# Attention's low parts stored apart and added later by DMA; the last bias of the fourth token block added in PSUM

## The chip, the core and the metric

The kernel runs on one core of a Trainium2 chip. Its engines are TensorE (PE, matmuls; PEld is its weight load), VectorE (DVE), ScalarE (ACT), GpSimd (POOL) and SyncE (SP, which only issues DMAs here). Each engine works through its own instructions in program order, and semaphores hold it where it needs what another has made. POOL issues DMAs as well, in line with its own arithmetic. Matmul results go to PSUM; everything else lies in SBUF, which DMAs fill from device memory.

The metric is the time of one execution on the device, in microseconds (us). Lower is better.

## The reference

One decoder layer in fp32, 512 tokens of width 2048, 16 query heads of 64 on 4 key heads, window 128:

```python
h = rms_norm(x, norm_gain[i])
z = h @ w_in[i]
q, k, v, g_attn, c_b, c_c, c_h, g_conv = jnp.split(z, SPLITS, axis=-1)
...
y_attn = sliding_window_attention(q, k, v, attn_sinks[i]) * jax.nn.silu(g_attn)
y_conv = c_b * short_conv(c_c * c_h, conv_w[i]) * jax.nn.silu(g_conv)
mix = jnp.concatenate([y_attn, y_conv], axis=-1)
x = x + mix @ w_out[i]
gate = jax.nn.sigmoid(rms_norm(x, ple_gate_norm_gain[i]) @ w_ple_gate[i] + b_ple_gate[i])
e = rms_norm(p[i] @ w_ple_proj[i], ple_norm_gain[i])
x = x + gate * e
```

Two places matter here: the sum of probabilities times values inside the attention, and the last line with the gate's bias `b_ple_gate`.

## The kernel before

**Precision.** Every fp32 operand is split into a high half, rounded to fp32r, and a low half, the rest. A product is three fp32r matmuls: high by high, low by high, high by low. `halves` makes a split: a cast on ACT (L199) and a subtraction on DVE (L200). The weight blocks so split are called wh and wl.

**Weight groups.** Most of the matrix work runs as nine groups g = 0 to 8 of `PER` = 28 steps, each step twelve 128x512 matmuls at L241: g 0 to 4 make the parts of the input projection (2 and 3 for the convolution, 4 for the attention's gate), 5 and 6 the output projection, 7 and 8 the gate of the per-layer embedding. A group computes a 2x2 product of blocks with seven products in place of eight, so weight blocks are first added to one another, on DVE (L189, L191) or by accumulating DMAs of POOL (L169). `run_step` does a step: the actions put in the table `before` for that step, the sums and splits of weight blocks ahead (`prepare(s + 2)`: two steps ahead, three pairs of buffers), the matmuls, the actions in the table `after`. `soon(table, s, fn, ...)` enters an action. That order of the code is the order of the engines.

**Attention.** It runs between 127 and 280 us, mixed with the matmuls of the remaining projections. `gemm_tile` (L712) calls `tick()` after every six of its matmuls, and `at(when, fn)` says at which tick a piece of the attention is issued. There are sixteen units, key head j by token block n. A unit's pieces are `scores` at its tick (matmuls L814 and L815, maxima and small 128x4 arithmetic on DVE, exponentials on ACT at L833), `turn` four ticks later (PE transposes the probabilities at L842, `halves` makes pth and ptl, and two POOL selects at L849 make the masked copies pph and ppl), `values` seven ticks later (four matmuls L859 onto pso, with pth, ptl, pph, ppl in that order), and one more twelve ticks later. In `values` ACT copies pso to `up`. Its upper 64 rows hold the product with the values' high halves and its lower 64 rows that with the low halves. POOL stores the upper rows to `attn_dram` (tiles a, L863); at tick 12 of the unit POOL issues a store of the lower rows that accumulates on the same place (L864). Five ticks ahead of every second unit `turn_q` turns the queries: PE transposes, `halves` makes `st` and `low`, and three POOL DMAs (L795 to L797) copy 64-row halves across partitions.

The result in `attn_dram` is first read in group 4, from step 18, by the loads of raw (563.8 to 587.7 us).

**The last two groups.** `token_scale`, in group 7 after its step 3, makes `r_2`, the reciprocal rms of each token: a sum and a scale on DVE (L309, L310), a power on POOL (L303). `gate_group` takes results out of PSUM (`take` L1294 on ACT, `join` L1302 on DVE), adds the bias, takes the sigmoid, multiplies by e (`times_e`, L1320), adds x2 and stores. In group 8 the block (t, n) = (1, 0), 128-token halves b = 0 and 1, comes last. Its products lie in two PSUM banks called pst. Its bias is added by `whole` (L1305): bank times r_2 plus gb, on DVE, in one 128x512 for b = 0 and two 128x256 for b = 1 (`tail`). Then come the sigmoid (L1382), `times_e`, the addition of x2 (L1375) and the store (L1376). The last two steps run all products of the first token half ahead of those of the second, with `first_block` (b = 0) between. `eps_tok` is a 128x4 tile that the attention stage uses and nothing reads later.

Where the program is written out, the scheduler keeps each engine's order in the weight groups as the tables give it. In the attention stage PE's order is by hand, and the other engines' order follows from what is ready.

Of the kernel before, what the change touches and what calls it, by code (L numbers as in the profile page):

```python
# [9 lines left out]
F32 = mybir.dt.float32  # L10
F32R = mybir.dt.float32r
AF = mybir.ActivationFunctionType
ALU = mybir.AluOpType
# [22 lines left out]
def hymba_layer(ctx: ExitStack, tc: tile.TileContext, io):  # L36
# [300 lines left out]
        soon(before, s0 + 21, lambda: join(qs[1, 1], g, "a", ALU.subtract))  # L337
        soon(after, s0 + 26, lambda: join(qs[0, 0], g, "c", ALU.add))

    attn_dram = [dram.tile([2 * P, T], F32, name=f"a{j}") for j in range(NKV)]  # L340
    conv_dram = [dram.tile([P, T], F32, name=f"c{i}") for i in range(4)]
    mix_dram = [dram.tile([P, T], F32, name=f"m{i}") for i in range(8)]
    tap_dram = [dram.tile([T, T], F32, name=f"t{i}") for i in range(3)]
# [439 lines left out]
    def turn_q(j, t):  # L783


        pt = ps_m.tile([P, T], F32, name="psm")
        for b in range(2):
            for f in range(2):
                s = j % 2 * 2 * P + f * P
                i = 2 * b + f  # L790
                nc.tensor.transpose(pt[:, i * P : (i + 1) * P], qs[t, j // 2][:, b, s : s + P], ident)
        st, st2 = (rowp.tile([P, T], F32R, tag="rows", name="st") for _ in range(2))
        low = misc.tile([P, T], F32R, tag="m", name="low")
        halves(st, low, pt)
        nc.gpsimd.dma_start(st2[:HD], st[HD:])  # L795
        nc.gpsimd.dma_start(st2[HD:], low[HD:])
        nc.gpsimd.dma_start(st[HD:], low[:HD])  # L797
        turned[j, t, 0], turned[j, t, 1] = st, st2

    turned = {}  # L800

    def attention(j, n, when):
# [52 lines left out]
        def values():  # L855
            po = ps_o.tile([P, 4, P], F32, name="pso")
            for i, (w, x) in enumerate(cell["pt"]):
                w = w.rearrange("p s d -> p (s d)")
                nc.tensor.matmul(po, w, x, start=i == 0, stop=i == len(cell["pt"]) - 1)  # L859
            up = mtile("up").rearrange("p (r t) -> p r t", t=P)  # L860
            nc.scalar.copy(up, po)
            rows = attn_dram[j].rearrange("(r d) (n t) -> d r n t", d=HD, n=NB)[:, :, n]
            nc.gpsimd.dma_start(rows, up[:HD])  # L863
            cell["add"] = lambda: nc.gpsimd.dma_start(rows, up[HD:], accum_op=ALU.add)  # L864

        if n % 2 == 0:
            at(when - 5, lambda: turn_q(j, n // 2))
        at(when, scores)
        at(when + 4, turn)
        at(when + 7, values)  # L870
        at(when + 12, lambda: cell["add"]())


    pgs = []
# [254 lines left out]
    def load_raw(j, src):  # L1129
        new_pair(mixf, j, move=j == 4)  # L1130
        for i in range(2):
            nc.sync.dma_start(pairs[id(mixf), j][0][i], src[(2 * j + i) % 8])

    attn_tiles = [attn_dram[i // 2][i % 2 * P : (i % 2 + 1) * P] for i in range(8)]

    def attn_group(g):
# [130 lines left out]
    for t in range(2):  # L1267
        soon(after, s1 + 5 + t, reload, t, 1)

    r_2, n_2 = [], []  # L1270

    def token_scale():
        r_2.append(inv_rms(x2sq, "x2"))
        n_2.append(const.tile([P, NB], F32, name="nr_x2"))
        nc.gpsimd.tensor_scalar(n_2[0], r_2[0], -1.0, None, op0=ALU.mult)

    soon(after, s2 + 3, token_scale)


    out = io["out"].rearrange("b p n -> p b n")  # L1280

    def gate_group(g):
        s0 = g * PER
        q, ext = {}, {}

        def load_b():
            ext["b"] = itile("gb")
            nc.sync.dma_start(ext["b"], io["b_ple_gate"][2 * (g - 7)][:, 0])

        def take(t, n, acc, r):  # L1290
# [10 lines left out]
            for b in range(2):  # L1301
                stt(z[:, b], psum[g, acc][b], column(r[0], t, b), z[:, b], op0=ALU.mult, op1=ALU.add)  # L1302

        def whole(t, n, b, cols=slice(0, T)):
            stt(  # L1305
                q[t, n][:, b, cols], psum[g, "a"][b][:, cols], column(r_2[0], t, b), ext["b"][:, cols],
                op0=ALU.mult, op1=ALU.add,
            )

        def load_e(t, n, tile=itile):  # L1310
            ext[t, n] = [tile("e") for _ in range(2)]
# [34 lines left out]
        soon(before, s0 + 21, join, 1, 1, "a", n_2)  # L1346
        finish(1, 1, s0 + 21)
        finish(0, 1, s0 + 20)
        soon(after, s0 + 22, load_b)
        soon(after, s0 + 22, load_e, 0, 0, itile if g == 7 else spare)  # L1350

        def new_z():
            q[1, 0] = qtile("z")

        if g == 7:
            soon(after, s0 + 26, join, 0, 0, "c", r_2)
            soon(after, s0 + 28, new_z)
            for b in range(2):
                soon(after, s0 + 28, whole, 1, 0, b)
            finish(0, 0, s0 + 28)  # L1360
            soon(after, s0 + 29, load_e, 1, 0)
            finish(1, 0, s0 + 31)
            return
# [3 lines left out]
            for b in range(2):  # L1367
                nc.sync.dma_start(ext["x2", t, n][b], x2_dram[t][2 + n][:, b])

        def piece(t, n, b, cols=slice(0, T), begun=False):  # L1370
            z = q[t, n][:, b, cols]
            if not begun:
                nc.scalar.activation(z, z, AF.Sigmoid)
            times_e(t, n, b, cols)
            tt(z, z, ext["x2", t, n][b][:, cols], op=ALU.add)  # L1375
            nc.sync.dma_start(part(out, t, 2 + n)[:, b, cols], z)  # L1376

        def tail(b, parts):
            cols = [slice(h * T // parts, (h + 1) * T // parts) for h in range(parts)]
            for c in cols:  # L1380
                whole(1, 0, b, c)
                nc.scalar.activation(q[1, 0][:, b, c], q[1, 0][:, b, c], AF.Sigmoid)  # L1382
            for c in cols:
                piece(1, 0, b, c, True)

        def first_block():
            new_z()
            tail(0, 1)

        soon(after, s0 + 21, load_x2, 0, 0)  # L1390
        soon(after, s0 + 22, load_x2, 1, 0)
        soon(after, s0 + 24, load_e, 1, 0, spare)
        soon(after, s0 + 24, join, 0, 0, "c", r_2)
        for b in range(2):
            soon(after, s0 + 25, piece, 0, 0, b)
        tail_work.append(first_block)
        soon(after, s0 + 27, tail, 1, 2)

    for g in T3_BY_DMA:
        for i, c in enumerate(chunks[g]):  # L1400
# [145 lines left out]
```

## Time and profile before

| | us |
|---|---|
| median of 3 runs | 914.39 (913.33 to 915.92) |
| profiled execution, device time | 912.85 |
| its span, first to last instruction | 911.1 |
| mean granted clock of PE | 0.998 |
| attention stage | 127 to 280 |
| last matmul starts | 904.51 |

Times below are counted from the start of the span. A page row of the engines gives busy time, its share and the number of instructions. A row of the timeline gives start, duration, engine, line, operation, output and inputs, and in brackets how long the engine had been idle before it and who released it. A row of waits gives the waiting instruction, who released it, and the sum in us, the number and the longest of such waits. "DMA x<-y" as a releaser is the landing of that transfer. Matmuls are pipelined: their recorded durations overlap, and their spacing is what one costs.

### The profile page before, as it was taken

To read this page: it belongs to the slowest core of one execution; us is meant where nothing else is said; L and a number is where in the kernel's file an instruction comes from. 1 tells how busy PE (TensorE), PEld (TensorE's weight loads), DVE (VectorE), ACT (ScalarE), POOL (GpSimd) and SP (SyncE) were. 2 spreads that over 40 slices of the span, in tenths; PEclk is the share of its full clock that TensorE was granted. 3 is DMA by queue.
4 is the path that set the end of the run, shared out by engine and by line. 5 is a ranking of instruction groups with operands and counts; after the bars stand their busy time and mean duration, and the time that the engine had idled before them with its cause. 6 is when DMAs were issued, how large, how long until landed. Compare 5 with 4: busy or idle time off the path is not lost.

```text
span 911.1 us, 11967 instructions
## 1 busy us (share of the span) xinstructions
PE 900.5 (99%) x4130; PEld 746.3 (82%) x4130; DVE 714.1 (78%) x967; ACT 527.7 (58%) x849; POOL 193.0 (21%) x264
## 2 busy tenths in 40 slices
PE   9999999999999999999999999999999999999997
PEld 7888888887878888888888888888888888888885
DVE  6878889887757687877768678997858887799678
ACT  6766848676653443454344457766556666665453
POOL 4232143376640001100130110012120112111100
PEclk9999999999999999999999999999999999999999
DMA  8999558756668858648478897858996995898647
GB/s 312 360 292 308 212 61 274 246 112 133 151 130 310 288 173 237 179 147 257 126 201 247 222 237 257 234 127 230 341 293 198 212 293 142 234 306 256 185 139 219
DMA packets 74445, 202.34 MB, mean 222 GB/s; under 512 B 8867, under 2 KB 15331, under 8 KB 74384
## 3 DMA queue, kind: packets, MB, share of 16 engines
q1 hardware_dynamic: 48672, 134.24, 43.1%
q0 software_dynamic: 25568, 67.33, 33.0%
q8 instruction: 32, 0.52, 0.2%
q14 instruction: 29, 0.24, 0.1%
q10 hardware_dynamic: 144, 0.01, 0.0%
HBM read 166.94 MB, written 31.46 MB: 218 GB/s over the span
## 4 chain that ended last, share of the span: by engine, by line
PE 86%; DVE 5%; issue 2%; ACT 2%; DMA 2%; POOL 2%; SPq 0%; DVEq 0%; POOLq 0%; ACTq 0%
PE psp L241 68%; PE psg L712 4%; PE pst L241 4%; PE psp L520 3%; PE pst L1024 2%; PE pss L900 1%; PE pst L1422 1%; PE pst L900 1%; DMA raw<-in_w_kv 1%; DVE wl L200 1%; DVE z L1320 1%; PE pso L859 1%; DMA st<-st 1%; DVE ptl L200 0%; DMA a<-up 0%
## 5 line engine op out<-in xcount | busy, mean ns | idle before, releaser
L241 PE MATMUL psp<-wh,form 128*128 128x512 f32 x1280 | 395.3, 390 | 0.0
L241 PEld LDWEIGHTS psp<-wh,form 128*128 128x128 f32 x1280 | 239.4, 188 | 49.2
L241 PE MATMUL psp<-wl,form 128*128 128x512 f32 x640 | 249.4, 390 | 0.0
L200 DVE TENSOR_TENSOR wl<-wy,wh 128x1024 fp32r<-128x1024 f32 x108 | 131.5, 1221 | 58.6 <-ACT wh L199 57.9
L199 ACT CAST wh<-wy 128x1024 fp32r<-128x1024 f32 x108 | 113.4, 1051 | 91.6 <-PE psp L241 72.4
L241 PEld LDWEIGHTS psp<-wl,form 128*128 128x128 f32 x640 | 120.1, 188 | 25.8 <-DVE wl L200 0.8
L200 DVE TENSOR_TENSOR wl<-wx,wh 128x1024 fp32r<-128x1024 f32 x72 | 87.9, 1222 | 51.2 <-ACT wh L199 51.1
L199 ACT CAST wh<-ws 128x1024 fp32r<-128x1024 f32 x72 | 75.8, 1053 | 74.0 <-PE psp L241 53.0
L241 PE MATMUL psp<-wh,hsh 128*128 128x512 f32 x304 | 118.6, 390 | 0.0
L241 PE MATMUL psp<-wl,hsh 128*128 128x512 f32 x304 | 118.3, 389 | 0.0
L241 PE MATMUL psp<-wh,hsl 128*128 128x512 f32 x304 | 118.3, 389 | 0.0
L199 ACT CAST wh<-wx 128x1024 fp32r<-128x1024 f32 x72 | 75.6, 1052 | 70.9 <-PE psp L241 49.9
L200 DVE TENSOR_TENSOR wl<-ws,wh 128x1024 fp32r<-128x1024 f32 x72 | 88.0, 1222 | 29.2 <-ACT wh L199 28.9
L189 DVE TENSOR_TENSOR wy<-wy,ws 128x1024 f32<-128x1024 f32 x72 | 87.6, 1217 | 0.0
L241 PEld LDWEIGHTS psp<-wl,hsh 128*128 128x128 f32 x304 | 57.1, 188 | 11.9
L241 PEld LDWEIGHTS psp<-wh,hsl 128*128 128x128 f32 x304 | 57.1, 188 | 11.8
L241 PEld LDWEIGHTS psp<-wh,hsh 128*128 128x128 f32 x304 | 57.1, 188 | 11.7
L712 PE MATMUL psg<-hsh,wh 128*128 128x512 f32 x112 | 45.3, 405 | 0.0
L712 PE MATMUL psg<-hsh,wl 128*128 128x512 f32 x112 | 43.8, 391 | 0.0
L712 PE MATMUL psg<-hsl,wh 128*128 128x512 f32 x112 | 43.8, 391 | 0.0
L169 POOL DMA_DIRECT2D wy<-in_w_mid x16 | 14.0, 876 | 136.9 <-DVE wy L189 83.3
L199 ACT CAST wh<-raw 128x1024 fp32r<-128x1024 f32 (+1 forms) x29 | 29.1, 1005 | 19.7 <-DMA raw<-in_w_ple_proj 6.9
(236 smaller groups left out, 1332.1 us busy)
## 6 DMA issues: line engine op xcount, KB each, us to landing
ws<-in_w_mid SPq DMA_DIRECT2D x40, 512.0 KB, 4.5
wx<-in_w_mid SPq DMA_DIRECT2D x24, 512.0 KB, 4.4
wy<-in_w_mid SPq DMA_DIRECT2D x20, 512.0 KB, 6.1
h<-form POOLq DMA_DIRECT2D x32, 256.0 KB, 5.7
wy<-in_w_mid POOLq DMA_DIRECT2D x16, 512.0 KB, 8.8
raw<-in_w_in SPq DMA_DIRECT2D x16, 512.0 KB, 4.6
wx<-in_w_out SPq DMA_DIRECT2D x16, 512.0 KB, 6.7
ws<-in_w_out SPq DMA_DIRECT2D x16, 512.0 KB, 6.2
```

Of the source, the lines that this page charges most:

```text
L169: nc.gpsimd.dma_start(t, w[n, r, j, c], accum_op=ALU.add)
L189: tt(y, y, got[g, "s1" if f == 6 else "s0", c], op=ALU.add)
L199: nc.scalar.copy(h, src)
L200: tt(l, src, f32(h), op=ALU.subtract)
L241: nc.tensor.matmul(ps[t], a, w[:, i], start=start and first and i == 0 and n == 0, stop=last and i == 1 and n == 2, skip_group_check=not s ...
L520: nc.tensor.matmul(kv_ps[t // 2][:, t % 2], hs[k][a][:, t * P : (t + 1) * P], kv_split[c][w][:, i], start=k == 0 and n == 0, stop=k == KT ...
L712: nc.tensor.matmul(ps, w[:, k % 8], a, start=k == 0 and n == 0, stop=k == KT - 1 and n == 2)
L859: nc.tensor.matmul(po, w, x, start=i == 0, stop=i == len(cell["pt"]) - 1)
L900: nc.tensor.matmul(banks[t], a, w[:, k], start=k == 0 and i == 0, stop=k == 1 and i == 2)
L1024: nc.tensor.transpose(pt[:, b], quads[b // 2][:, b % 2, f * P : (f + 1) * P], ident)
L1320: stt(z[:, b, cols], z[:, b, cols], column(r_e, t, b), ext[t, n][b][:, cols], op0=ALU.mult, op1=ALU.mult)
L1422: nc.tensor.matmul(ps, w[:, k % 8], a, start=k == 0 and n == 0, stop=k == KT - 1 and n == 2)
```

## The change

1. **Attention's low halves** go to an array of their own, `low_dram` (tiles l), by a plain store right behind that of the high halves, in `values`; the accumulating store at tick 12 is gone. In group 2, after steps 4, 9, 14 and 19, POOL issues one accumulating DMA each (`add_low`), which adds the whole of l to a for one key head: 1024x128, memory to memory.
2. **The third copy of `turn_q`** is issued one tick later.
3. **Group 8's last block**: the bias of its half b = 1 is added in PSUM, as gb divided by r_2, on DVE before step 21 (`bias_first`), while products are still to be accumulated there. The sigmoid then reads the bank and scales by r_2, so the two 128x256 `whole` are gone. The quotient needs the reciprocal of r_2, made by a DVE instruction in `token_scale` and kept in `eps_tok`.
4. **Loads**: gb, x2 and e of group 8's last blocks are loaded after steps 15 to 19 into tiles that finished steps leave free (`spare`).

```diff
--- before.py
+++ after.py
@@ -337,7 +337,7 @@
         soon(before, s0 + 21, lambda: join(qs[1, 1], g, "a", ALU.subtract))
         soon(after, s0 + 26, lambda: join(qs[0, 0], g, "c", ALU.add))
 
-    attn_dram = [dram.tile([2 * P, T], F32, name=f"a{j}") for j in range(NKV)]
+    attn_dram, low_dram = ([dram.tile([2 * P, T], F32, name=f"{x}{j}") for j in range(NKV)] for x in "al")
     conv_dram = [dram.tile([P, T], F32, name=f"c{i}") for i in range(4)]
     mix_dram = [dram.tile([P, T], F32, name=f"m{i}") for i in range(8)]
     tap_dram = [dram.tile([T, T], F32, name=f"t{i}") for i in range(3)]
@@ -794,8 +794,8 @@
         halves(st, low, pt)
         nc.gpsimd.dma_start(st2[:HD], st[HD:])
         nc.gpsimd.dma_start(st2[HD:], low[HD:])
-        nc.gpsimd.dma_start(st[HD:], low[:HD])
         turned[j, t, 0], turned[j, t, 1] = st, st2
+        return lambda: nc.gpsimd.dma_start(st[HD:], low[:HD])
 
     turned = {}
 
@@ -859,16 +859,16 @@
                 nc.tensor.matmul(po, w, x, start=i == 0, stop=i == len(cell["pt"]) - 1)
             up = mtile("up").rearrange("p (r t) -> p r t", t=P)
             nc.scalar.copy(up, po)
-            rows = attn_dram[j].rearrange("(r d) (n t) -> d r n t", d=HD, n=NB)[:, :, n]
-            nc.gpsimd.dma_start(rows, up[:HD])
-            cell["add"] = lambda: nc.gpsimd.dma_start(rows, up[HD:], accum_op=ALU.add)
+            for i, x in enumerate((attn_dram, low_dram)):
+                rows = x[j].rearrange("(r d) (n t) -> d r n t", d=HD, n=NB)[:, :, n]
+                nc.gpsimd.dma_start(rows, up[i * HD : (i + 1) * HD])
 
         if n % 2 == 0:
-            at(when - 5, lambda: turn_q(j, n // 2))
+            at(when - 5, lambda: cell.update(last=turn_q(j, n // 2)))
+            at(when - 4, lambda: cell["last"]())
         at(when, scores)
         at(when + 4, turn)
         at(when + 7, values)
-        at(when + 12, lambda: cell["add"]())
 
 
     pgs = []
@@ -1130,6 +1130,12 @@
         new_pair(mixf, j, move=j == 4)
         for i in range(2):
             nc.sync.dma_start(pairs[id(mixf), j][0][i], src[(2 * j + i) % 8])
+
+    def add_low(j):
+        nc.gpsimd.dma_start(attn_dram[j], low_dram[j], accum_op=ALU.add, max_dma_last_dim=T)
+
+    for j in range(NKV):
+        soon(after, 2 * PER + 4 + 5 * j, add_low, j)
 
     attn_tiles = [attn_dram[i // 2][i % 2 * P : (i % 2 + 1) * P] for i in range(8)]
 
@@ -1267,12 +1273,14 @@
     for t in range(2):
         soon(after, s1 + 5 + t, reload, t, 1)
 
-    r_2, n_2 = [], []
+    r_2, n_2, over_r2 = [], [], []
 
     def token_scale():
         r_2.append(inv_rms(x2sq, "x2"))
         n_2.append(const.tile([P, NB], F32, name="nr_x2"))
         nc.gpsimd.tensor_scalar(n_2[0], r_2[0], -1.0, None, op0=ALU.mult)
+        over_r2.append(eps_tok)
+        nc.vector.reciprocal(over_r2[0], r_2[0])
 
     soon(after, s2 + 3, token_scale)
 
@@ -1283,8 +1291,8 @@
         s0 = g * PER
         q, ext = {}, {}
 
-        def load_b():
-            ext["b"] = itile("gb")
+        def load_b(tile=itile):
+            ext["b"] = tile("gb")
             nc.sync.dma_start(ext["b"], io["b_ple_gate"][2 * (g - 7)][:, 0])
 
         def take(t, n, acc, r):
@@ -1301,11 +1309,12 @@
             for b in range(2):
                 stt(z[:, b], psum[g, acc][b], column(r[0], t, b), z[:, b], op0=ALU.mult, op1=ALU.add)
 
-        def whole(t, n, b, cols=slice(0, T)):
-            stt(
-                q[t, n][:, b, cols], psum[g, "a"][b][:, cols], column(r_2[0], t, b), ext["b"][:, cols],
-                op0=ALU.mult, op1=ALU.add,
-            )
+        def whole(t, n, b):
+            stt(q[t, n][:, b], psum[g, "a"][b], column(r_2[0], t, b), ext["b"], op0=ALU.mult, op1=ALU.add)
+
+        def bias_first():
+            ps = psum[g, "a"][1]
+            stt(ps, ext["b"], column(over_r2[0], 1, 1), ps, op0=ALU.mult, op1=ALU.add)
 
         def load_e(t, n, tile=itile):
             ext[t, n] = [tile("e") for _ in range(2)]
@@ -1346,13 +1355,13 @@
         soon(before, s0 + 21, join, 1, 1, "a", n_2)
         finish(1, 1, s0 + 21)
         finish(0, 1, s0 + 20)
-        soon(after, s0 + 22, load_b)
-        soon(after, s0 + 22, load_e, 0, 0, itile if g == 7 else spare)
 
         def new_z():
             q[1, 0] = qtile("z")
 
         if g == 7:
+            soon(after, s0 + 22, load_b)
+            soon(after, s0 + 22, load_e, 0, 0)
             soon(after, s0 + 26, join, 0, 0, "c", r_2)
             soon(after, s0 + 28, new_z)
             for b in range(2):
@@ -1367,34 +1376,41 @@
             for b in range(2):
                 nc.sync.dma_start(ext["x2", t, n][b], x2_dram[t][2 + n][:, b])
 
-        def piece(t, n, b, cols=slice(0, T), begun=False):
+        def finish_part(t, n, b, cols=slice(0, T)):
             z = q[t, n][:, b, cols]
-            if not begun:
-                nc.scalar.activation(z, z, AF.Sigmoid)
             times_e(t, n, b, cols)
             tt(z, z, ext["x2", t, n][b][:, cols], op=ALU.add)
             nc.sync.dma_start(part(out, t, 2 + n)[:, b, cols], z)
 
-        def tail(b, parts):
-            cols = [slice(h * T // parts, (h + 1) * T // parts) for h in range(parts)]
+        def piece(b):
+            z = q[0, 0][:, b]
+            nc.scalar.activation(z, z, AF.Sigmoid)
+            finish_part(0, 0, b)
+
+        def last_block():
+            cols = [slice(h * T // 2, (h + 1) * T // 2) for h in range(2)]
             for c in cols:
-                whole(1, 0, b, c)
-                nc.scalar.activation(q[1, 0][:, b, c], q[1, 0][:, b, c], AF.Sigmoid)
+                nc.scalar.activation(
+                    q[1, 0][:, 1, c], psum[g, "a"][1][:, c], AF.Sigmoid, scale=column(r_2[0], 1, 1))
             for c in cols:
-                piece(1, 0, b, c, True)
+                finish_part(1, 0, 1, c)
 
         def first_block():
             new_z()
-            tail(0, 1)
-
-        soon(after, s0 + 21, load_x2, 0, 0)
-        soon(after, s0 + 22, load_x2, 1, 0)
-        soon(after, s0 + 24, load_e, 1, 0, spare)
+            whole(1, 0, 0)
+            nc.scalar.activation(q[1, 0][:, 0], q[1, 0][:, 0], AF.Sigmoid)
+            finish_part(1, 0, 0)
+
+        soon(after, s0 + 15, load_b, spare)
+        for i, fn in enumerate((load_x2, load_e)):
+            for t in range(2):
+                soon(after, s0 + 16 + 2 * i + t, fn, t, 0, *(spare,) * i)
+        soon(before, s0 + 21, bias_first)
         soon(after, s0 + 24, join, 0, 0, "c", r_2)
         for b in range(2):
-            soon(after, s0 + 25, piece, 0, 0, b)
+            soon(after, s0 + 25, piece, b)
         tail_work.append(first_block)
-        soon(after, s0 + 27, tail, 1, 2)
+        soon(after, s0 + 27, last_block)
 
     for g in T3_BY_DMA:
         for i, c in enumerate(chunks[g]):
```

The order of the instructions on POOL in the attention stage, around the matmuls at 209 to 212 us. Names: a and l are the two arrays (with a number for the key head), st and low the turned queries. Before:

```order
L849 AFFINE_SELECT pph<-pth 128x512
L797 DMA st<-low 64x512
L849 AFFINE_SELECT ppl<-ptl 128x512
L864 DMA a_85<-up 64x4x128
L795 DMA st<-st 64x512
L796 DMA st<-low 64x512
L797 DMA st<-low 64x512
L863 DMA a_85<-up 64x4x128
L849 AFFINE_SELECT pph<-pth 128x512
L864 DMA a_85<-up 64x4x128
L849 AFFINE_SELECT ppl<-ptl 128x512
```

And in the changed kernel, the same stretch:

```order
L795 DMA st<-st 64x512
L796 DMA st<-low 64x512
L798 DMA st<-low 64x512
L864 DMA a_85<-up 64x4x128
L864 DMA l_89<-up 64x4x128
L849 AFFINE_SELECT pph<-pth 128x512
L864 DMA a_86<-up 64x4x128
L849 AFFINE_SELECT ppl<-ptl 128x512
L864 DMA l_90<-up 64x4x128
```

The accumulating store between pph and ppl (L864 before) is gone, and plain stores of a and l, both at L864 now, stand around the selects.

POOL in group 2 of the changed kernel, where t<-z are stores of the convolution's taps and wy<-in_w_mid the accumulating loads of weight blocks:

```order
L169 DMA wy<-in_w_mid 128x1024
L1056 DMA t_103<-z 128x2x512
L1135 DMA a_83<-l_87 1024x128
L1056 DMA t_105<-z 128x2x512
L1056 DMA t_104<-z 128x2x512
L1135 DMA a_84<-l_88 1024x128
L1056 DMA t_103<-z 128x2x512
L1135 DMA a_85<-l_89 1024x128
L1135 DMA a_86<-l_90 1024x128
L169 DMA wy<-in_w_mid 128x1024 x4
```

The four rows L1135 are new. All three accumulating loads that stand ahead of them in this group keep their place, and the next four follow behind them. In the kernel before, the last t<-z is issued at 384.97 and the next L169 at 419.64.

DVE in `token_scale` and behind it, in the changed kernel:

```order
L309 TENSOR_REDUCE ms<-x2sq 128x4
L310 TENSOR_SCALAR ms<-ms 128x4
L1283 RECIPROCAL eps_tok<-r_x_7054 128x4
L200 TENSOR_TENSOR wl<-wx,wh 128x1024
L977 SCALAR_TENSOR_TENSOR g<-raw,g 128x256
L978 SCALAR_TENSOR_TENSOR g<-raw,g 128x256
```

Only the reciprocal is new there. In group 8 the one row of `bias_first` comes between the join on pst and a sum of weight blocks, and at the end the two `whole` are missing:

```order
L1310 SCALAR_TENSOR_TENSOR z<-pst,nr_x_7056,z 128x512 x2
L1317 SCALAR_TENSOR_TENSOR pst<-gb,eps_tok,pst 128x512
L189 TENSOR_TENSOR wy<-wy,ws_7816 128x1024
L200 TENSOR_TENSOR wl<-wy,wh 128x1024
L1329 SCALAR_TENSOR_TENSOR z<-z,r_e,e 128x512 x2
```

Everything else on DVE, and all of PE, stands in the order of before.

## The prediction

> **What bounds the kernel now.** I read the page first: the busy line, the chain that ended last, and the list of DMA issues (line and queue, number, KB each, median us to landing).
>
> ```profile
> PE 900.5 (99%) x4130; PEld 746.3 (82%) x4130; DVE 714.1 (78%) x967; ACT 527.7 (58%) x849; POOL 193.0 (21%) x264
> PE 86%; DVE 5%; issue 2%; ACT 2%; DMA 2%; POOL 2%; SPq 0%; DVEq 0%; POOLq 0%; ACTq 0%
> wy<-in_w_mid POOLq DMA_DIRECT2D x16, 512.0 KB, 8.8
> ```
>
> TensorE (PE) is busy for 900.5 of 911.1 us and carries 86% of the chain. The change leaves every matmul in place, so only two things can move the end: an idle stretch of PE that goes or comes, and the work behind the last matmul. The view of waits says where PE waits within the reach of the change, and for what its releaser had waited (sum, times, longest):
>
> ```profile
> PE pso L859 <- POOL ppl L849: 1.8, 1, 1.8
> PE pso L859 <- POOL pph L849: 0.6, 1, 0.6
> PE pss L814 <- DMA st<-low: 0.4, 1, 0.4
> POOL a L864 <- DMA a<-up: 24.3, 12, 4.3
> ```
>
> All three PE waits lie in the attention stage. The fourth row is the reason behind the first two: twelve times POOL stands 24.3 us in all before an accumulating store L864, until the plain store L863 of the same rows has landed. The timeline of PE shows the places (start, duration, instruction, wait before it):
>
> ```profile
> 200.57 0.35 PE L814 MATMUL pss<-khh,st 128*128 128x256 f32 x1 [0.41 <-DMA st<-low]
> 202.99 0.60 PE L842 MATMUL pst<-ident,prob 128*128 128x128 f32 x4
> ...
> 209.20 0.39 PE L859 MATMUL pso<-ptl,vv 128*128 128x512 f32 x1
> 209.43 0.39 PE L859 MATMUL pso<-pph,vd 128*128 128x512 f32 x1
> 211.59 0.50 PE L859 MATMUL pso<-ppl,vd 128*128 128x512 f32 x1 [1.78 <-POOL ppl L849]
> ...
> 265.76 0.39 PE L859 MATMUL pso<-ptl,vv 128*128 128x512 f32 x1
> 266.75 0.49 PE L859 MATMUL pso<-pph,vd 128*128 128x512 f32 x1 [0.60 <-POOL pph L849]
> 267.33 0.50 PE L859 MATMUL pso<-ppl,vd 128*128 128x512 f32 x1
> ```
>
> Undisturbed, these matmuls start 0.23 apart (209.20 to 209.43). The late one at 211.59 lost 211.59 − 209.43 − 0.23 = 1.93. Those at 266.75 and 267.33 lost 0.76 and 0.35.
>
> **Part 1, the low halves stored apart.** The POOL timeline holds, in order, the instructions that fed those matmuls:
>
> ```profile
> 206.29 0.66 POOL L849 TENSOR_SCALAR_AFFINE_SELECT pph<-pth 128x512 fp32r<-128x512 f32 x1
> 209.82 1.06 POOL L864 DMA_DIRECT2D a<-up  x1 [2.87 <-DMA a<-up]
> 210.49 1.05 POOL L849 TENSOR_SCALAR_AFFINE_SELECT ppl<-ptl 128x512 fp32r<-128x512 f32 x1
> ...
> 264.34 1.06 POOL L864 DMA_DIRECT2D a<-up  x1 [3.83 <-DMA a<-up]
> 265.64 1.05 POOL L849 TENSOR_SCALAR_AFFINE_SELECT pph<-pth 128x512 fp32r<-128x512 f32 x1
> ```
>
> Between pph and ppl of the first unit stands one accumulating store, held 2.87; it is now a plain store of another array, which waits for nothing that lands. Priced at 1.06 (the issue at 264.34), it lets ppl start at 206.29 + 0.66 + 1.06 = 208.0 and end by 209.1; PE would want it at 209.43 + 0.23 = 209.66. The wait goes, with 0.6 to spare. For the last unit the inputs decide:
>
> ```profile
> 262.52 0.58 ACT L199 CAST pth<-pst 128x512 fp32r<-128x512 f32 x1
> 263.31 0.68 DVE L200 TENSOR_TENSOR ptl<-pst,pth 128x512 fp32r<-128x512 f32 x1
> 202.84 0.19 ACT L833 ACTIVATION_READ_ACCUMULATOR prob<-prob,negms,msq 128x1 f32 x1
> ```
>
> The first ends at 263.10, the second at 263.99. With POOL free, pph is done by 264.2 and ppl by 265.1, both before PE asks (265.99 and 266.22). So 1.93 + 0.76 + 0.35 = **3.04** can go. The moved `st<-low` copy would free 0.41 more at 200.57, but the transposes at 202.99 follow exponentials whose last row ends at 202.84 + 0.19 = 203.03: PE cannot come there earlier, so I count that wait at nothing. It is ACT that would be late next. I take −3.04 for part 1.
>
> Whether the stage keeps all of it hangs on VectorE (DVE), which makes the softmax's small tiles:
>
> ```profile
> 215.99 1.20 DVE L831 SCALAR_TENSOR_TENSOR negms<-negms,nsink 128x4 f32<-128x4 f32 x1
> 258.36 0.78 DVE L831 SCALAR_TENSOR_TENSOR negms<-negms,nsink 128x4 f32<-128x4 f32 x1
> 764.96 0.17 DVE L310 TENSOR_SCALAR ms<-ms 128x4 f32<-128x4 f32 x1
> ```
>
> A 128x4 instruction should take some 0.17. The two L831 lost 1.03 and 0.61 beside POOL's L849. If the freed POOL no longer meets them, up to 1.64 more goes; if it meets others, part comes back. Both ends are kept.
>
> The additions moved to group 2 are four POOL transfers of 512 KB, memory to memory. No row shows one. Below: nothing, as POOL and the queue are free behind them. Above: the loads ahead of a product are late by one whole transfer, 8.8 by the list above (the same size on the same queue). What they could delay is here (ACT cast of a weight block that had waited for its load, DVE low part, first matmul that reads it):
>
> ```profile
> 372.19 2.00 ACT L199 CAST wh<-wy 128x1024 fp32r<-128x1024 f32 x2 [1.71 <-DMA wy<-in_w_mid]
> 373.27 1.23 DVE L200 TENSOR_TENSOR wl<-wy,wh 128x1024 fp32r<-128x1024 f32 x1 [0.40 <-ACT wh L199]
> 375.58 0.39 PE L241 MATMUL psp<-wl,form 128*128 128x512 f32 x1
> ```
>
> The block is ready at 374.50 and read at 375.58: slack 1.08. I take nothing, since the loads of these blocks are issued ahead of the first addition, which takes its place on the queue behind them.
>
> By the Trainium skill, DMA: Bandwidth & Descriptors, section "Anatomy of one DMA — SWDGE (gpsimd) path", a transfer from this queue costs about 2.0 us plus bytes over 436 GB/s, which I estimate at 3.2 us for 524,288 bytes. The 8.8 above is far over it, so the trace does not bear the rule out beside other loads; by it the delay would be at most 3.2 − 1.08 = 2.1, leaving −1.2 where the upper end would leave a loss.
>
> **Part 2, the reciprocal.** DVE gets one new 128x4 instruction, in token_scale, between ms (764.96) and the low part of a weight block (765.06). It waits for POOL's power:
>
> ```profile
> 765.06 1.22 DVE L200 TENSOR_TENSOR wl<-wx,wh 128x1024 fp32r<-128x1024 f32 x1
> 768.81 1.22 DVE L200 TENSOR_TENSOR wl<-wy,wh 128x1024 fp32r<-128x1024 f32 x1
> 171.60 1.04 POOL L303 TENSOR_TENSOR r_e<-ms,half_neg 128x4 f32<-128x4 f32 x1
> 765.21 1.99 POOL L303 TENSOR_TENSOR r_x<-ms,half_neg 128x4 f32<-128x4 f32 x1 [10.42 <-DVE ms L310]
> 771.63 0.39 PE L241 MATMUL psp<-wl,form 128*128 128x512 f32 x1
> ```
>
> Behind it stand the weight splits that PE reads. The power took 1.99 while the DVE block of 765.06 ran, 1.04 elsewhere. DVE now stands still meanwhile, so I take 1.04: power done at 766.25, reciprocal 0.17, DVE late by 766.42 − 765.06 = 1.36. The tightest block behind it ends at 770.03 and is read at 771.63, slack 1.60: nothing reaches PE. With 1.99 the delay is 2.31 and PE waits 2.31 − 1.60 = 0.71, call it 0.8 with a semaphore.
>
> The Trainium skill, SBUF — State Buffer, section "Who interferes with whom", says that a DVE instruction with two SBUF inputs and a GpSimd instruction that reads SBUF exclude each other, the first holding the shared ports for its whole length. The pair 765.06/765.21 agrees (1.99 against 1.04). By that rule the power runs at 1.04 once DVE waits for it, and the term is 0; without it, +0.8.
>
> **Part 3, the bias in PSUM and the end.** DVE's rows around the new instruction and at the end, with the matmul that reads the second of the two blocks behind it:
>
> ```profile
> 885.18 1.47 DVE L1302 SCALAR_TENSOR_TENSOR z<-pst,nr_x,z 128x512 f32<-128x512 f32 x2
> 894.89 2.35 DVE L200 TENSOR_TENSOR wl<-wy,wh 128x1024 fp32r<-128x1024 f32 x2
> 897.03 0.39 PE L241 MATMUL pst<-wl,form 128*128 128x512 f32 x1
> 904.63 0.69 DVE L1375 TENSOR_TENSOR z<-z,xb 128x512 f32<-128x512 f32 x1
> 905.24 0.87 DVE L1305 SCALAR_TENSOR_TENSOR z<-pst,r_x,gb 128x256 f32<-128x256 f32 x2
> 906.20 0.48 DVE L1320 SCALAR_TENSOR_TENSOR z<-z,r_e,e 128x256 f32<-128x256 f32 x1
> ```
>
> The bias costs one 128x512 on PSUM behind 885.18. Two of that kind took 1.47, so one is 0.74. DVE's timeline has no pause from there to the end of its weight blocks, so everything behind shifts by 0.74. The tightest block, the first of the pair at 894.89, ends half way, at 896.07, and is read at 897.03: slack 0.96, so PE keeps its time. At the end the two L1305 go, and the sigmoid on ACT reads PSUM itself. DVE's last 128x512, after which the first L1305 began at 905.24, would then free it at 905.24 + 0.74 = 905.98, where before the next work started at 906.20: **−0.22**. The moved loads of gb, x2 and e cost nothing on SP: in its program all of them stand behind the last weight load, and before the stores.
>
> **Sum.** −3.04 + 0 + 0 − 0.22 = −3.3. The profiled execution took 912.85 and would take 909.55. It stands 1.54 under the median of 914.39, so on the scale of the median I forecast **911.1**. A measurement of this kernel can tell about 0.3%, or 2.74 us, from no change: the forecast lies just beyond it.
>
> **The rivals.**
> - *The stalls of L831 go as well.* POOL runs its selects earlier, off DVE's small tiles: −3.3 − 1.4 (most of 1.64) = −4.7, 909.7. For it: both rows lie beside an L849. Against it: as many selects run as before, in other places. Chance 0.14.
> - *The reciprocal holds the splits.* The power takes 1.99 although DVE waits: −3.3 + 0.8 = −2.5, 911.9. Against it stand the two rows of 1.04. Chance 0.12.
> - *The waits change place.* PE, 1.93 earlier, comes before the exponentials (203.03 against 202.99 shows how close) and gives that back; only the last unit, behind which there is none, keeps 0.76 + 0.35, with 0.22 at the end: −1.3, 913.1. This is also the case in which the change does not do what it says. Chance 0.17.
> - *Slower: the additions collide.* The 512 KB additions push the weight loads of group 2 back by a whole 8.8. PE loses 8.8 − 1.08 = 7.7 against 3.3 won: +4.4, 918.8. It turns the sign from a delay of 3.3 + 1.08 = 4.4 on, and is measurable from 7.1. For it: a cast waits 1.71 for such a load already. Against it: they are issued behind these loads. Chance 0.07.
>
> **How the numbers follow.** The forecast has the remaining 0.50. Faster by over 0.3%: nearly all of the first rival (0.13), most of the forecast (0.40, as its size is uncertain by about a microsecond), a quarter of the reciprocal case (0.03): 0.56. Slower by over 0.3%: 0.07. Within it: 0.37. The range runs from 909.4, a little under the first rival, to 914.0, a microsecond over the changed places; it leaves out the slow case and the tails.
>
> **What would show it.** Right: no PE wait for ppl or pph at L859, no POOL wait for a landing in attention, DVE held about 1.4 in token_scale without a PE pause behind it, DVE starting the last half block at once. Wrong: new PE waits for prob (exponentials), PE pauses for wl near 372 or 771, or a weight block behind the bias that comes after 897.03.

## The result and the profile after

| | before | changed |
|---|---|---|
| median, us (range, runs) | 914.66 (912.13 to 915.92, 6) | 909.59 (909.02 to 909.91, 6) |
| profiled execution, us | 912.85 | 909.47 |
| its span, us | 911.1 | 907.8 |

The ratio of the times is 0.9947, with a 95% interval of 0.9933 to 0.9962: faster by 0.5%. The profiled executions differ by 3.4 us, the medians by 5.1, and the times of the kernel before scatter over 3.8 us where those of the changed kernel stay within 0.9. The experiments come back to both.

First the waits of PE in the changed kernel, the whole list (who waited, for whom, sum in us, times, longest):

```profile
PE pst L368 <- DVE zeros L364: 1.1, 1, 1.1
PE pso L859 <- POOL ppl L849: 0.5, 1, 0.5
PE pst L842 <- ACT prob L833: 0.2, 1, 0.2
```

The first stands at the start of the program in both kernels. The 1.8 for ppl, the 0.6 for pph and the 0.4 for st<-low are gone; a wait for ppl of 0.5 and one for the exponentials of 0.2 are new. The timeline of PE, at the places shown for before:

```profile
199.57 0.28 PE L814 MATMUL pss<-khh,st 128*128 128x256 f32 x1
...
201.91 1.32 PE L842 MATMUL pst<-ident,prob 128*128 128x128 f32 x4
...
208.85 0.39 PE L859 MATMUL pso<-ptl,vv 128*128 128x512 f32 x1
...
209.30 0.39 PE L859 MATMUL pso<-ppl,vd 128*128 128x512 f32 x1
...
233.32 0.39 PE L859 MATMUL pso<-pph,vd 128*128 128x512 f32 x1
234.16 0.50 PE L859 MATMUL pso<-ppl,vd 128*128 128x512 f32 x1 [0.45 <-POOL ppl L849]
...
264.04 0.39 PE L859 MATMUL pso<-ptl,vv 128*128 128x512 f32 x1
...
264.49 0.39 PE L859 MATMUL pso<-ppl,vd 128*128 128x512 f32 x1
...
901.47 0.39 PE L241 MATMUL pst<-wl,form 128*128 128x512 f32 x1
```

Each row set against the same matmul of before tells where PE moved. At 208.85 (209.20 before) it is 0.35 earlier, and has been since the first 35 us of the program, where nothing was changed. At 209.30 (211.59) it is 2.29 earlier: the 1.93 went. At 264.04 (265.76) only 1.72 is left: the new wait at 234.16, 0.84 behind its neighbour instead of 0.23, took 0.61. At 264.49 (267.33) it is 2.84: 0.76 and 0.35 went. The last matmul is 3.04 earlier (901.47 for 904.51).

At 199.57 (200.57) it is 1.00 earlier, that is 0.65 more than the 0.35. This was given back at once: the four transposes that took 0.60 take 1.32, since the exponentials are not ready. The new wait at 234 has its reason on POOL and DVE:

```profile
231.15 0.66 POOL L864 DMA_DIRECT2D l<-up  x1 [1.07 <-issue]
231.81 0.65 POOL L849 TENSOR_SCALAR_AFFINE_SELECT pph<-pth 128x512 fp32r<-128x512 f32 x1
232.40 1.71 POOL L849 TENSOR_SCALAR_AFFINE_SELECT ppl<-ptl 128x512 fp32r<-128x512 f32 x1
```

```profile
232.41 1.21 DVE L200 TENSOR_TENSOR wl<-raw,wh 128x1024 fp32r<-128x1024 f32 x1
```

The select takes 1.71 where its neighbour takes 0.65, and DVE's split of a weight block lies upon it. The Trainium skill, SBUF — State Buffer, section "Who interferes with whom", says that two such instructions exclude each other; the trace agrees that one of them waits (1.71 against 0.65 for the select, 1.21 as ever for the split), though two starts 0.01 apart don't tell which came first.

DVE in token_scale (first fence) and at the end (second):

```profile
761.95 0.17 DVE L310 TENSOR_SCALAR ms<-ms 128x4 f32<-128x4 f32 x1
763.28 0.18 DVE L1283 RECIPROCAL eps_tok<-r_x 128x4 f32<-128x4 f32 x1 [1.16 <-POOL r_x L303]
763.39 1.22 DVE L200 TENSOR_TENSOR wl<-wx,wh 128x1024 fp32r<-128x1024 f32 x1
```

```profile
883.50 0.75 DVE L1317 SCALAR_TENSOR_TENSOR pst<-gb,eps_tok,pst 128x512 f32<-128x512 f32 x1
884.15 1.22 DVE L189 TENSOR_TENSOR wy<-wy,ws 128x1024 f32<-128x1024 f32 x1
...
902.83 0.48 DVE L1329 SCALAR_TENSOR_TENSOR z<-z,r_e,e 128x256 f32<-128x256 f32 x1
```

DVE stands 1.16 in token_scale, and PE has no wait behind it. The bias took 0.65 of DVE's time, and the last half block begins at 902.83 without a pause: 3.37 earlier than 906.20, that is 0.33 more than PE's 3.04.

### The profile page after: what moved, and what is told of

Same layout as the page of the kernel before. It is cut to its first block, busy times and chain, and to the rows that moved or that the text cites. A ratio compares the mean times of both kernels' runs of the same rounds, so it can differ in the third digit from the quotient of the medians.

```text
span 907.8 us, 11969 instructions
## 1 busy us (share of the span) xinstructions
PE 899.7 (99%) x4130; PEld 747.0 (82%) x4130; DVE 713.6 (79%) x967; ACT 527.6 (58%) x849; POOL 191.6 (21%) x268
## 4 chain that ended last, share of the span: by engine, by line
PE 72%; DVE 4%; ACT 2%; issue 1%; POOL 0%; DMA 0%; DVEq 0%; ACTq 0%
PE psp L241 60%; PE psg L712 4%; PE pst L241 4%; PE pst L1024 2%; PE pst L1438 1%; PE pso L859 1%; DVE wl L200 1%; ACT prob L833 1%; DVE z L1329 0%; PE pst L842 0%; PE pss L815 0%; PE pss L814 0%; DVE wy L189 0%; ACT z L1030 0%; DVE rope L413 0%
## 5 line engine op out<-in xcount | busy, mean ns | idle before, releaser
L169 POOL DMA_DIRECT2D wy<-in_w_mid x16 | 14.1, 879 | 134.5 <-DVE wy L189 80.7
L833 ACT ACTIVATE prob<-prob,negms,msq 128x128 f32<-128x128 f32 x64 | 30.9, 483 | 16.8 <-DVE negms L831 16.8
```

Source lines behind the costliest of these rows:

```text
L169: nc.gpsimd.dma_start(t, w[n, r, j, c], accum_op=ALU.add)
L833: nc.scalar.activation(t[:, r], t[:, r], AF.Exp, scale=r_q[:, r : r + 1], bias=negm[:, r : r + 1], accum_out=sums[:, r : r + 1],)
```

## The experiments

Each ratio is against the kernel before, run beside it on the same chip.

| run | median, us (range, runs) | ratio (95% interval) |
|---|---|---|
| low_only | 909.69 (909.06 to 910.97, 12) | 0.9959 (0.9945 to 0.9973) |
| low_no_turn | 909.86 (909.03 to 911.27, 12) | 0.9960 (0.9944 to 0.9977) |
| tail_only | 911.93 (910.41 to 918.08, 12) | 0.9994 (0.9974 to 1.0014) |
| wait_only | 908.55 (908.22 to 909.43, 6) | 0.9943 (0.9924 to 0.9962) |
| add_prev | 913.75 (911.92 to 915.01, 11) | 1.0012 (0.9998 to 1.0026) |
| copies_sp | 910.26 (909.55 to 911.23, 12) | 0.9971 (0.9956 to 0.9986) |
| no_adds | 909.63 (908.96 to 910.26, 7) | 0.9956 (0.9938 to 0.9974) |
| adds_at0 | 922.79 (922.14 to 923.23, 4) | 1.0097 (1.0073 to 1.0120) |
| recip_slow | 911.97 (911.46 to 913.53, 10) | 0.9983 (0.9969 to 0.9998) |
| low_sp | 909.00 (908.15 to 909.71, 7) | 0.9964 (0.9950 to 0.9979) |
| low_at8 | 907.83 (907.60 to 909.65, 5) | 0.9961 (0.9949 to 0.9974) |

The kernel before in the four sets of these runs: 913.80 (910.83 to 920.15, 29 runs), 913.45 (18 runs), 912.74 (17) and 912.69 (17). Against the larger samples the medians are 3 to 4 us apart; the 5.1 of the first comparison came from a sample of six that lay high.

### One part at a time

low_only is the kernel before with the parts 1 and 2 of the change, tail_only with 3 and 4, low_no_turn with part 1.

> The kernel before with the attention part alone (low halves stored apart, added in group 2, third query copy one tick later); bias, reciprocal and loads as before. Theory (POOL's waits for landed stores held PE): the PE waits for ppl and pph at 211 and 266 go, PE is 2.6 us earlier behind the attention stage, and the medians differ from before by nearly all of the 4.9 us of the whole change (ratio about 0.995). Rival (the gain sits in the last group): no change here, ratio 1.000. Second rival (the profiled gain of 3.3 is this part, and what the medians show beyond it is the tail's): ratio about 0.997.

> The kernel before with the last group's part alone (bias in PSUM, reciprocal, loads at steps 15 to 19); attention as before. Theory: 0.2 to 0.3 us, under what can be measured (ratio 0.9997, interval over 1), DVE's last half block 0.2 to 0.3 closer behind the last matmul. Rival (the tail carries what the medians show beyond the profile): about 1.5 us, ratio 0.998.

> The attention part without the later third query copy. Theory (that copy's wait is hidden behind ACT's exponentials): the same time as with it within 0.3 us; a PE wait for st<-low near 200 may come back at 0.4 to 0.6, given back at the transposes near 203. Rival: the copy's place counts, 0.4 to 0.6 us slower behind the attention stage.

> The kernel before once more, for a second profile. If the spread of its times (912.1 to 915.9 against 909.0 to 909.9 of the changed kernel) comes from POOL's waits for landed stores, the waits of PE at L859 and L814 in attention have another sum here than 2.8 us, and the span differs by that. If it comes from elsewhere (start of the program, weight loads), the three waits are the same and PE's shift arises at other places.

low_only has the whole gain that times can show, and the narrow range. tail_only can't be told from before, and keeps before's wide range; its 0.2 to 0.3 is too small to be shown by times. The later third copy changes nothing that can be measured (909.86 without it against 909.69 with it). The gain and the calm both belong to the attention's stores.

old_1 took 912.47. Its PE waits in attention:

```profile
PE pso L859 <- POOL ppl L849: 0.5, 2, 0.3
PE pss L814 <- DMA st<-low: 0.5, 1, 0.5
PE pso L859 <- POOL pph L849: 0.3, 1, 0.3
```

The same program, and the waits lie elsewhere: the 1.8 has become two of at most 0.3, and the three sum to 1.3 where before they sum to 2.8. Yet the span is only 0.3 shorter (910.8 against 911.1). Set against the profile of before, PE is 1.5 further ahead behind 211 us, and has given 1.1 of it back at two places, near 224 and 245 us. So the waits of the attention change place from one execution to the next, but this pair of profiles does not show that they make the scatter. What speaks for it is that the scatter shrinks in low_only and stays in tail_only. That a run of 916 or 920 loses its time at these places was not seen: none of them was profiled.

### What in the old stores costs: the wait or the addition

The prediction's reason was POOL's wait for the landing of the first store. wait_only keeps the wait and takes the addition out of the second transfer:

```diff
-            cell["add"] = lambda: nc.gpsimd.dma_start(rows, up[HD:], accum_op=ALU.add)
+            cell["add"] = lambda: nc.gpsimd.dma_start(rows, up[HD:])
```

> The kernel before, with the second store of each unit made a plain one that overwrites the high half's rows: the low halves are left out of the attention. POOL's instructions and their order are the same, and so is the wait for the landing of the first store; only the addition is gone from the transfer. Theory (the wait for the landing is what costs): as slow and as spread as before, ratio 1.000, 12 waits of some 24 us in all on POOL. Rival (the accumulating transfer itself costs, 1.06 us of POOL against 0.62 for a plain one and a later landing): most of the gain comes without moving anything, ratio about 0.996.

The theory fell. POOL's waits for landed stores in wait_only, and then the only wait of PE beside the one for zeros (this one lies at 23 us, far ahead of the attention):

```profile
POOL a L864 <- DMA a<-up: 19.1, 9, 3.7
```

```profile
PE psp L520 <- ACT hsh L199: 0.4, 1, 0.4
```

POOL still stands 19.1 us, and PE has no wait left in attention. At the two places of the prediction, the store between pph and ppl that was held 2.87 is not held at all now (206.39), and the one ahead of the last pph is held 2.76 in place of 3.83 and harms nothing. So taking the addition out is enough for the gain, and a wait for a landing need not cost PE anything. add_prev was meant as the opposite corner: all sixteen additions, on rows that landed long ago.

```diff
+            stored.append(rows)
+            to = stored[max(len(stored) - 4, 0)]
-            cell["add"] = lambda: nc.gpsimd.dma_start(rows, up[HD:], accum_op=ALU.add)
+            cell["add"] = lambda: nc.gpsimd.dma_start(to, up[HD:], accum_op=ALU.add)
```

> The kernel before, with each accumulating store put on the rows of the unit three earlier, which landed long ago: the low halves go to wrong token blocks. As many accumulations as before, but POOL need not wait for a store that it has just issued. Runs so far: wait with a plain second store 908.6, no wait and plain stores 909.6, wait with accumulation 913.5 to 914.7. Theory A (it takes both: an accumulation that lands late and a POOL that waits for landings): the waits of L866 for a<-up go, PE's waits at L859 go, about 909.5 with a narrow spread, ratio 0.995 to 0.996. Theory B (the accumulations alone delay what stands behind them, copies of the queries and selects): about as slow and as spread as before, ratio over 0.998.

The time is the one that theory B expected, 913.75, and so is the spread. But the trace does not bear theory B out. POOL's wait for the copies between 180 and 280 us in add_prev, then POOL's rows around 196 us, and PE's rows behind them:

```profile
POOL st L797 <- DMA st<-st: 9.6, 6, 3.0
```

```profile
192.85 1.09 POOL L866 DMA_DIRECT2D a<-up  x1
196.53 1.03 POOL L866 DMA_DIRECT2D a<-up  x1 [2.59 <-DMA a<-up]
...
198.91 1.07 POOL L849 TENSOR_SCALAR_AFFINE_SELECT pph<-pth 128x512 fp32r<-128x512 f32 x1
200.65 0.54 POOL L797 DMA_DIRECT2D st<-low  x1 [0.66 <-DMA st<-st]
201.19 0.66 POOL L849 TENSOR_SCALAR_AFFINE_SELECT ppl<-ptl 128x512 fp32r<-128x512 f32 x1
```

```profile
200.04 0.49 PE L859 MATMUL pso<-pph,vd 128*128 128x512 f32 x1 [0.46 <-POOL pph L849]
201.90 0.50 PE L859 MATMUL pso<-ppl,vd 128*128 128x512 f32 x1 [1.36 <-POOL ppl L849]
203.06 0.35 PE L814 MATMUL pss<-khh,st 128*128 128x256 f32 x1 [0.65 <-DMA st<-low]
```

The index `max(len(stored) - 4, 0)` sends the first four additions to the same rows, so the second, at 196.53, waits 2.59 for the first, issued at 192.85, to land. Right behind that wait PE loses some 3.2 us in three steps (200.04, 201.90 and 203.06), where the same matmuls of wait_only follow 0.23 apart. The 0.9 that it loses at 236 stands behind POOL's wait of 3.0 for a copy. Elsewhere in attention it loses nothing, although additions go on there. So this run does not have the addition without a wait: theory B is not shown, and theory A, that it takes both, is not refuted.

What the corners do show: with wait and addition 912.7 to 914.7, with the wait and no addition 908.55, with neither 909.59. Taking the addition out is what brings the gain. Whether taking out the waits alone would bring it too stays open. In the trace of before the additions land 3.2, 3.5 and 4.9 us after their issue (least, median, most); the plain second stores of wait_only land after 2.4, 2.5 and 4.5. What comes behind one suffers too. The POOL timeline of before:

```profile
199.33 1.13 POOL L864 DMA_DIRECT2D a<-up  x1
200.02 1.00 POOL L795 DMA_DIRECT2D st<-st  x1
202.27 0.51 POOL L796 DMA_DIRECT2D st<-low  x1 [1.25 <-DVE low L200]
205.14 0.51 POOL L797 DMA_DIRECT2D st<-low  x1 [2.35 <-DMA st<-st]
205.64 0.65 POOL L863 DMA_DIRECT2D a<-up  x1
```

and the same instructions in wait_only:

```profile
198.28 0.66 POOL L864 DMA_DIRECT2D a<-up  x1
198.93 0.53 POOL L795 DMA_DIRECT2D st<-st  x1
202.14 0.53 POOL L796 DMA_DIRECT2D st<-low  x1 [2.68 <-DVE low L200]
202.66 0.52 POOL L797 DMA_DIRECT2D st<-low  x1
203.67 0.65 POOL L863 DMA_DIRECT2D a<-up  x1 [0.49 <-ACT up L861]
...
206.39 0.64 POOL L864 DMA_DIRECT2D a<-up  x1
```

Behind the addition at 199.33 the copy st<-st lands so late that the third copy waits 2.35 for it, the next store is issued at 205.64 instead of 203.67, the addition behind that waits for it until 209.82 (in wait_only the store at 206.39 finds it landed), and ppl, and PE at 211.59, wait for POOL. That is the chain of which the prediction read only the last link, the 2.87.

copies_sp asks how much of it goes by the query copies: in the kernel before it puts the three of them on SP's queue.

```diff
-        nc.gpsimd.dma_start(st2[:HD], st[HD:])
-        nc.gpsimd.dma_start(st2[HD:], low[HD:])
-        nc.gpsimd.dma_start(st[HD:], low[:HD])
+        nc.sync.dma_start(f32(st2[:HD]), f32(st[HD:]))
+        nc.sync.dma_start(f32(st2[HD:]), f32(low[HD:]))
+        nc.sync.dma_start(f32(st[HD:]), f32(low[:HD]))
```

> The kernel before with the three query copies of turn_q on SP's queue in place of POOL's; both stores of each unit stay on POOL, the second still accumulating and waiting for the first. What is open: by which way an accumulation reaches PE. Theory Q (through the queue: the copies stand behind accumulations, land late, and POOL waits for them): 909 to 910.5, POOL's waits at the third copy gone, PE's waits at L814 and L859 mostly gone. Theory S (through POOL itself: selects take 0.86 in the mean against 0.65 and the second store waits for the first): the waits of PE for ppl and pph stay, 912 to 914. Rival to both (SP waits for the copies' inputs and its weight loads come late): PE waits for blocks of L712, slower than 914.

POOL's wait for its own stores there, and PE's wait in attention:

```profile
POOL a L864 <- DMA a<-up: 27.1, 12, 4.7
```

```profile
PE pso L859 <- POOL ppl L849: 0.7, 1, 0.7
```

The time is theory Q's: 910.26 against 912.69 beside it, so moving the copies brings about 2.4 us and a range of 1.7, while POOL waits longer than ever for its stores (27.1). But theory S has a part too. Set against wait_only, PE loses 1.9 us between 258 and 266, first at this wait and then behind selects of 1.05 in place of 0.65. The move also takes the copies' issues and waits off POOL, so how much of the 2.4 is their late landing and how much is a freer POOL is not taken apart.

### The additions in group 2

no_adds leaves the four additions out; adds_at0 puts them ahead of a load (`soon(after, 2 * PER + 0, add_low, j)`).

> The changed kernel without the four additions in group 2: the low halves are stored, but left out of the result. Theory (the additions are hidden, although each takes 9 to 16 us to land): the time of the changed kernel, 909.6 within 0.3 us. Rival (they slow the weight loads of group 2 a little): up to 1 us faster.

> The changed kernel with all four additions issued after step 0 of group 2, so that they stand on POOL ahead of the last accumulating load of a weight block there. Theory (the additions are harmless only because they stand behind these loads): four issues of 1.4 us hold that load back by about 3 us, and the 2 MB ahead of it in the queue by more; with a slack of 1.08 PE waits for a wl near 372 and the time rises by 3 to 10 us. Rival (the transfers do not hinder each other, the slack is larger than it looks): no change.

no_adds is level with the changed kernel (909.63 and 909.59, not run side by side): the additions cost nothing that can be measured where they stand. Their landing in the changed kernel, and PE's longest wait in adds_at0:

```profile
DMA to landing us min/median/max: 9.0/11.3/15.6
```

```profile
PE psp L241 <- ACT wh L199: 10.2, 1, 10.2
```

In the changed kernel each lands 9.0 to 15.6 us after its issue, above the 8.8 that the prediction took as its upper bound. The Trainium skill's page DMA: Bandwidth & Descriptors, "Anatomy of one DMA — SWDGE (gpsimd) path", gave an estimate of 3.2, which the trace does not bear out for these transfers.

Ahead of the load they cost 13 us (922.79 against 909.63 beside it), more than the 3 to 10 expected: it is their place on the queue that makes them free. The load was not issued later for it (360.96, in the changed kernel 361.16), as the expectation had thought; it landed 19.3 us after its issue, where in the changed kernel no load there took more than 8.2. Beside the wait of 10.2, PE lost another 2.9 us behind it: between 380 and 386 us its granted clock was 0.54, and its matmuls started up to 0.66 apart instead of 0.23.

### The reciprocal

recip_slow adds two powers on POOL ahead of it (`power(r_2[0], eps_tok)`, twice).

> The changed kernel with two more powers on POOL between the one that makes r_2 and the reciprocal (their results are overwritten). DVE then stands some 2.3 us longer in token_scale, about 3.6 in all. Theory (PE's next tight block has 1.60 us of slack there, so that the 1.3 of the change cost nothing): PE waits for wl near 768, and the time rises by 3.6 - 1.6 = 2.0 us over the changed kernel. Rival (slack is made up elsewhere, DVE catches up): no change.

DVE's wait, and PE's:

```profile
765.78 0.18 DVE L1285 RECIPROCAL eps_tok<-r_x 128x4 f32<-128x4 f32 x1 [3.61 <-POOL eps_tok L303]
```

```profile
PE psp L241 <- DVE wl L200: 1.1, 1, 1.1
...
PE psp L241 <- DVE form L200: 0.4, 1, 0.4
```

DVE stood 3.61, PE waited twice, and the time is 911.97, 2.4 over the changed kernel and 2.3 over no_adds beside it, where 2.0 was expected. So the slack is about what was read, and the 1.16 of the change lies inside it.

### Towards a better version

low_sp puts the stores of l on SP's queue; low_at8 issues them one tick behind those of a (`at(when + 8, ...)`).

> The changed kernel with the stores of the low halves on SP's queue in place of POOL's, between its loads of weights. POOL loses 16 issues of 0.62 in attention. Theory (the PE wait of 0.5 for ppl near 234 in the changed kernel comes from a POOL that is 0.62 later there, so that the select meets a weight split on DVE and takes 1.71): that wait goes, about 0.5 us faster than the changed kernel, 909.1. Rival (SP waits for ACT's copies ahead of its weight loads, and a load is late): 0.5 to 2 us slower.

> The changed kernel with the store of the low halves issued one tick behind that of the high halves. The instructions stay the same; on POOL two selects move ahead of a store. Theory: the wait of PE for ppl near 234 changes by a few tenths at most, 909.3 to 909.8. Rival (the store ahead of the selects is what makes that wait): 0.5 us faster.

Both lose the wait at 234. low_sp has a new one of 0.4 for a weight block. In low_at8 the two selects stand ahead of the store of l:

```profile
229.58 0.65 POOL L849 TENSOR_SCALAR_AFFINE_SELECT pph<-pth 128x512 fp32r<-128x512 f32 x1
230.16 0.64 POOL L849 TENSOR_SCALAR_AFFINE_SELECT ppl<-ptl 128x512 fp32r<-128x512 f32 x1
230.86 0.65 POOL L865 DMA_DIRECT2D l<-up  x1
```

They are done before DVE's split begins, PE waits for nothing in attention, and the profiled span is 906.8, 1.0 under the changed kernel. The rival was right about its cause: with the select out of DVE's way PE gains 0.6 there, and the other 0.6 at the transposes of 202 us, less 0.2 lost elsewhere. The median is the lowest of all, 907.83, but it was not timed beside the changed kernel, and the intervals of the ratios overlap. That the wait is gone is shown; that the kernel is faster rests on one profile of each.

## Why the prediction was right, and where its reason was not

- **The time.** Forecast −3.3 on the profiled execution, 911.1 on the scale of the median; measured −3.4 and 909.59, close to the lower end of the range (909.4). The prediction shifted both kernels by the 1.54 between the profile of before and its median of three runs. That median lay high, above the 912.7 to 913.8 of the larger samples, and the changed kernel has no such distance (909.47 profiled, 909.59 median). That −3.4 came so near to −3.3 is in part luck: attention gave half a microsecond less than forecast, and 0.35 at the start of the program and 0.11 more at the end made up for it.
- **Part 1, −3.04.** The terms came as worked out: 1.93 at 211 and 1.11 at 266. In between 0.6 was lost to a collision of a select with a weight split, which the L831 paragraph had named as possible, at another instruction. The early 0.35 is no part of the change. Without it attention gave 2.84 − 0.35 = 2.5.
- **The reason for part 1** was read too short: "held 2.87 ... it is now a plain store of another array, which waits for nothing that lands". The place was right, and the wait does stand in front of ppl there. But wait_only keeps the wait for the own store, 19.1 us of it, and has the whole gain. What makes such waits long and late enough to reach PE are the accumulating transfers. The change removed both the additions and these waits, so the forecast held; whether removing the waits alone would have done it, no run shows.
- **The moved copy at nothing**: right, by PE's rows at 199.57 and 201.91 and by low_no_turn. Here the wait did change places, as the third rival said; at 211 and 266 it did not.
- **The additions at nothing**: right, for the reason given, their place behind the loads (no_adds and adds_at0). The upper bound of 8.8 for one of them was too low by 0.2 to 6.8, so the slower rival was priced too low, but its condition did not arise.
- **The reciprocal at nothing**: right. The power took 1.04 once DVE stood still, as taken; DVE was late by 763.39 − 761.95 less the 0.10 of before, that is 1.34 for a forecast of 1.36.
- **The end, −0.22**: −0.33. The term mis-sized is the bias, 0.65 of DVE's time in place of 0.74, and its sign and place were right.
- **The L831 stalls**: three of 0.50, 0.56 and 0.62 lie in the changed kernel (205.70, 231.93, 256.79), where before had 0.38, 1.20 and 0.78; they moved, and that rival did not come.
- **The signs.** Three of the signs named came out as for a wrong prediction: PE has a wait for ppl (0.5) and one for the exponentials (0.2), and POOL still waits for landings in attention, of copies (st<-st, 8.1 us in six waits, 7.8 in four before). The others came as for a right one.

## What to carry to other kernels

A wait in the profile names the last link: before it is taken for the cause, keep the wait and remove what makes it long, and the other way round. Then look in that run's own trace whether what was to go is gone at the place where the time is lost; in add_prev it was not. In this kernel an accumulating transfer was a cost for what stood behind it on its queue, and small ones in a latency-bound stage were better stored plainly and added later, in a place where nothing on that queue was due soon. And where a kernel's times scatter, one profile is one draw: look for waits on transfers, and compare medians over many runs.

## What the runs showed of the hardware that was not expected

- The accumulating stores of 64x4x128 landed a median 3.5 us after issue, plain ones of that shape 2.5, and POOL's selects behind them were stretched. The select of pph in before and in wait_only (least, median, most in ns):

```profile
L849 POOL TENSOR_SCALAR_AFFINE_SELECT pph<-pth x12: 634/955/1507, 183.3 to 265.6; 128x512 fp32r<-128x512 f32 x12
```

```profile
L849 POOL TENSOR_SCALAR_AFFINE_SELECT pph<-pth x12: 629/647/848, 183.4 to 261.9; 128x512 fp32r<-128x512 f32 x12
```

- Accumulating 512 KB from memory to memory took 9.0 to 15.6 us to land. Four in a row held back a load behind them on the same queue until PE stood 10.2 us; then PE ran at a granted clock of 0.54 for some 5 us, which cost 2.9 more.
- The kernel before, unchanged, took from 909.8 to 920.15 us; without accumulating stores in attention no version here spread over more than 2.3 us (4 to 12 runs each). copies_sp, which keeps these stores and moves the query copies to another queue, spread over 1.7.
